# The tail of a diffusion-step kernel: a reciprocal root from ScalarE's square root, and a product on VectorE

## The chip, the cores and the metric

The kernel runs on one core of a Trainium2 chip. A time is the device time of one execution in microseconds (us); a kernel's time is the median of its runs. A core has TensorE (matrix products into PSUM banks), VectorE, ScalarE and GpSimd (element by element, on tiles in SBUF), and SyncE, which issues transfers. Each engine has its own ordered queue of instructions and waits for the others by semaphores. In the profile they are PE, DVE, ACT, POOL and SP; PEld is TensorE's loading of weights.

## The reference

One layer of a diffusion backbone, in float32, for 128 context tokens and 1024 latent tokens with 1024 features. Attention heads and a matrix-memory head group stand side by side, then comes a SwiGLU block of 2816 hidden features, and at the very end a root-mean-square norm with a gain per feature:

```python
def rmsnorm(x, w):
    xf = x.astype(F32)
    y = xf * lax.rsqrt(jnp.mean(xf * xf, axis=-1, keepdims=True) + EPS)
    return (y * w.astype(F32)).astype(x.dtype)
...
    h2 = rmsnorm(x, norm2_w) * (1 + sc2) + sh2
    x = x + g2 * swiglu(h2, w_gu, w_down)
...
y_sample = rmsnorm(xs, final_norm_w)
```

The change touches the last of this, for the last tokens only: the gated sum `x + g2 * ...`, then the sum of its squares over a row, the reciprocal root, and the product with root and gain.

## The kernel before, in words

The 1152 tokens are nine blocks of 128 rows, in three chunks of three blocks (`CB` = 3). A chunk's rows lie in SBUF as `x1[0..2]`, each 128 x 1024. Projections, attention and the matrix memory come first; then each chunk goes through the SwiGLU block in groups of hidden features. For a group, `gate_up` makes 128 hidden features at a time, and `down` multiplies them into the rows and adds the gated result. Each factor is split into a high and a low part, so each product is three matmuls.

For the first two chunks the final norm is done by `finish`, beside the next chunk's matmuls. For the third chunk the last group (four times 128 hidden features) is `down_last`, which ends the program. For each block `i` of its three and each half row `n` of 512 features it does the following:

- twelve matmuls into one PSUM bank (L1391 to L1393);
- `add_gated`: on VectorE the product of the bank with the gate (L1104, `t`), then the sum into the row (L1105, `x`);
- on ScalarE the square of the half row with its sum in a column of `st` (L1397, `jk`; the profile shows a second instruction that reads the accumulator);
- after the first half only: on VectorE one column, sum/1024 + EPS (L1399, `st`), and on GpSimd the half row times the norm's gain `fw` (L1400).

After both halves `rsqrt` (L121 to L134) makes the reciprocal root of the mean square in twelve VectorE operations on one column: L127 forms the mean, L128 and L129 make a first guess from the bits of the number, and three rounds of L131, L132 and L133 are Newton steps. Then ScalarE scales the first half row, which has its gain already (L1403), and VectorE scales the second half and multiplies the gain in one operation (L1404). The first half leaves by a transfer issued from ScalarE's queue (L1405), the second by one from SyncE's (L1406).

The order of the instructions in each engine's queue is made by a planner when the program is built (`TC_OPTS`, L1498). It goes through the program with durations of its own, and lets an engine take what is ready, what stands earlier in the program (or was raised by `hot`) first. So the operations of three blocks are mixed on VectorE, and once the order is made, an engine keeps to it whatever the chip does.

Of the kernel before, what the change touches and what calls it, by code (L numbers as in the profile page):

```python
# [8 lines left out]
F32 = mybir.dt.float32  # L9
# [4 lines left out]
AF = mybir.ActivationFunctionType  # L14
ALU = mybir.AluOpType
# [4 lines left out]
P = 128  # L20
D = 1024
# [12 lines left out]
CB = 3  # L34
# [11 lines left out]
def hybrid_step(ctx: ExitStack, tc: tile.TileContext, I: dict, O: dict):  # L46
    nc = tc.nc
    mm = nc.tensor.matmul
    act = nc.scalar.activation
    dve = nc.vector  # L50
    pool = nc.gpsimd
# [6 lines left out]
    def nm(s):  # L58
        uid[0] += 1
        return f"{s}_{uid[0]}"  # L60
# [24 lines left out]
    def yrow(b):  # L85
        if b == 0:
            return O["y_prompt"][0]
        return O["y_sample"][0, (b - 1) * P : b * P, :]
# [14 lines left out]
    def bank():  # L103
        return psum["mm"].tile([P, 512], F32, name=nm("mm"), tag="mm")
# [16 lines left out]
    def rsqrt(tp, ss, n, inv, cap=16, plus=EPS):  # L121

        v = tp.tile([P, cap], F32, name=nm("rv"), tag="rv", bufs=2)[:, :n]
        y = tp.tile([P, cap], F32, name=nm("ry"), tag="ry", bufs=2)[:, :n]
        t = tp.tile([P, cap], F32, name=nm("rt"), tag="rt", bufs=2)[:, :n]
        h = tp.tile([P, cap], I32, name=nm("rh"), tag="rh", bufs=2)[:, :n]
        dve.tensor_scalar(out=v, in0=ss, scalar1=inv, scalar2=plus, op0=ALU.mult, op1=ALU.add)  # L127
        dve.tensor_scalar(out=h, in0=v.bitcast(I32), scalar1=1, scalar2=None, op0=ALU.logical_shift_right)  # L128
        dve.tensor_scalar(out=y.bitcast(I32), in0=h, scalar1=-1, scalar2=0x5F3759DF, op0=ALU.mult, op1=ALU.add)  # L129
        for _ in range(3):  # L130
            dve.tensor_tensor(out=t, in0=y, in1=y, op=ALU.mult)  # L131
            dve.scalar_tensor_tensor(out=t, in0=t, scalar=-0.5, in1=v, op0=ALU.mult, op1=ALU.mult)  # L132
            dve.scalar_tensor_tensor(out=y, in0=t, scalar=1.5, in1=y, op0=ALU.add, op1=ALU.mult)  # L133
        return y  # L134
# [4 lines left out]
    def load_piece(srcs, shape, raw=None, own=None):  # L139

        a, b = shape
        n = a * b

        def view(t):
            return t[:, :n].rearrange("p (a b) -> p a b", b=b)

        raw = raw or wp.tile([P, 1024], F32, name=nm("raw"), tag="raw", bufs=2)
        hi = own[0] if own else wp.tile([P, 1024], F32R, name=nm("whi"), tag="whi", bufs=5)
        lo = own[1] if own else wp.tile([P, 1024], F32R, name=nm("wlo"), tag="wlo", bufs=5)
        for part, ap_ in srcs:  # L150
            dma(part(view(raw)), ap_)
        nc.scalar.copy(hi[:, :n], raw[:, :n])  # L152
        sub(lo[:, :n], raw[:, :n], hi[:, :n].bitcast(F32), "dve")
        return view(hi), view(lo)
# [162 lines left out]
    for n in (1, 4):  # L317
        dve.tensor_scalar(out=bcol[:, n * KD : (n + 1) * KD], in0=bcol[:, n * KD : (n + 1) * KD],
                          scalar1=1.0, scalar2=None, op0=ALU.add)
# [781 lines left out]
    def add_gated(x1, ps, g, n, eng=dve):  # L1101
        cs = slice(n * 512, (n + 1) * 512)
        t = t2()
        dve.tensor_tensor(out=t, in0=ps, in1=g, op=ALU.mult)  # L1104
        eng.tensor_tensor(out=x1[:, cs], in0=x1[:, cs], in1=t, op=ALU.add)  # L1105
# [248 lines left out]
    def finish(c, a):  # L1354
# [6 lines left out]
        for i in range(CB):  # L1361
# [4 lines left out]
            dma(yrow(c * CB + i), x1[i])  # L1366
            yield

    def down_last(c, a, f0, nf):

        gs, ws = [], []
        fw = ap2.tile([P, D], F32, name="fw", tag="pr", bufs=2)
        dma(fw, I["final_norm_w"].rearrange("(o n) -> o n", o=1).to_broadcast([P, D]))
        for n in range(2):
            pieces = []
            for j in range(0, nf, 2):
                rows = w_down[(f0 + j) * P : (f0 + j + 2) * P, n * 512 : (n + 1) * 512].rearrange("(a p) n -> p a n", p=P)
                pieces.append(load_piece([(full_view, rows)], (2, 512)))
            ws.append(pieces)
            gl = ft.tile([P, 512], F32, name=nm("gl"), tag=("gl", "gx")[n], bufs=1)  # L1380
            dma(gl, g_d[1, 1:2, n * 512 : (n + 1) * 512].to_broadcast([P, 512]))
            gs.append(gl)
        for i in range(CB):
            sl = slice(i * P, (i + 1) * P)
            st = ap.tile([P, 4], F32, name=nm("st"), tag="st", bufs=4)
            for n in range(2):
                ps = bank()
                for k in range(nf):
                    wh, wl = ws[n][k // 2]
                    ah, al = a["act"][k][0][:, sl], a["act"][k][1][:, sl]  # L1390
                    mm(ps, ah, wh[:, k % 2, :], start=(k == 0), stop=False)  # L1391
                    mm(ps, ah, wl[:, k % 2, :], start=False, stop=False)
                    mm(ps, al, wh[:, k % 2, :], start=False, stop=(k == nf - 1))  # L1393
                add_gated(a["x1"][i], ps, gs[n], n)
                v = a["x1"][i][:, n * 512 : (n + 1) * 512]
                jk = ft.tile([P, D], BF16, name=nm("jk"), tag="t2", bufs=3)
                act(jk[:, 0:512], v, AF.Square, accum_out=st[:, n : n + 1])  # L1397
                if n == 0:
                    dve.tensor_scalar(out=st[:, 2:3], in0=st[:, 0:1], scalar1=1.0 / D, scalar2=EPS, op0=ALU.mult, op1=ALU.add)  # L1399
                    pool.tensor_tensor(out=v, in0=v, in1=fw[:, 0:512], op=ALU.mult)  # L1400
            r = rsqrt(fp, st[:, 1:2], 1, 1.0 / D, CB, st[:, 2:3])
            lo, hi = a["x1"][i][:, 0:512], a["x1"][i][:, 512:1024]
            act(lo, lo, AF.Copy, scale=r)  # L1403
            dve.scalar_tensor_tensor(out=hi, in0=hi, scalar=r, in1=fw[:, 512:1024], op0=ALU.mult, op1=ALU.mult)  # L1404
            nc.scalar.dma_start(yrow(c * CB + i)[:, 0:512], lo)  # L1405
            dma(yrow(c * CB + i)[:, 512:1024], hi)  # L1406
# [29 lines left out]
    fp = ctx.enter_context(tc.tile_pool(name="fp", bufs=1, side="right", reuse_waits="tile"))  # L1436
# [31 lines left out]
    for c in range(NCH):  # L1468
        if c + 1 < NCH:
            main = groups(c, cur, GROUPS[:NG])  # L1470
            for _ in range(4):
                next(main)
            weave(main, chain(previous(c, cur), att), 18 * sum(nf for _, nf in GROUPS[:NG]) - 24, 50)
            emit(att)
            attn_out(nxt, oT, out_gates())
            emit(groups(c, cur, GROUPS[NG:-1]))
            f0, nf = GROUPS[-1]
            emit(gate_up(cur, f0, nf))
            n2 = chain(*[norm2(c + 1, nxt, i) for i in range(CB)])
            weave(chain(down(c, cur, f0, nf, 0), down(c, cur, f0, nf, 1)), n2, 6 * nf, 8)  # L1480
            emit(n2)
            if c + 2 < NCH:
                oT = []
                att = attention(c + 2, oT, set())
            nxt["prev"] = cur
            cur = nxt
            nxt = cur["next"] = {}
        else:
            main = groups(c, cur, LAST[:-1])
            for _ in range(4):  # L1490
                next(main)
            weave(main, previous(c, cur), 24, 3)
            emit(main)
            emit(gate_up(cur, *LAST[-1]))
            down_last(c, cur, *LAST[-1])
# [52 lines left out]
```

## Time and profile before

| what | value |
|---|---|
| median of 3 runs | 1572.1 us (1570.31 to 1574.45) |
| the profiled execution, its own time | 1574.08 us |
| its span | 1572.3 us |
| granted TensorE clock, mean | 0.979 |
| busy: TensorE, VectorE, ScalarE, GpSimd | 95%, 65%, 49%, 17% of the span |

The span is the time from the first to the last event of the profile; the execution's own time is 1.8 us longer. A row of the timeline gives start, duration, engine, line of the kernel, operation, and output and input tiles with their shapes. Durations of neighbours on VectorE and ScalarE overlap a little, so the distance from one start to the next is the better measure of what an operation costs its queue. A row in the groups by line ends with busy time, mean nanoseconds of one instruction, and the idle time before them with what ended it.

### The profile page before, as it was taken

The page shows a single profiled execution, that of the slowest core. Times are in us where ns is not written, and L with a number is a line of the kernel's source. Part 1 is how long each engine was busy: PE and PEld are TensorE (multiplying, and loading weights), DVE is VectorE, ACT ScalarE, POOL GpSimd, SP SyncE. Part 2 cuts the span into 40 slices and gives each one's busy share as a digit, 9 for nine tenths or more (in the row PEclk, how much of TensorE's full clock was granted, in tenths as well). Part 3 has the DMA queues.
Part 4 walks back from the last instruction along what each step waited for, and adds up shares of the span by engine and source line. Part 5 has one row for each costly group of instructions (what it writes and reads, how often), then busy time and mean ns, then how long its engine had stood idle before and what let it go on. Part 6 is the DMA issues. An engine that isn't in the chain of part 4 may idle for free.

```text
span 1572.3 us, 23397 instructions
## 1 busy us (share of the span) xinstructions
PE 1487.7 (95%) x8539; PEld 1247.3 (79%) x8539; DVE 1022.9 (65%) x2025; ACT 771.8 (49%) x1409; POOL 271.4 (17%) x357
## 2 busy tenths in 40 slices
PE   6899999999999689999999999999999999999996
PEld 3544567676766468898998989989898989999995
DVE  4878554737659576677555677877866585554555
ACT  4754465847656344545432444556552443323332
POOL 0213333322343242100110101000010101001111
PEclk9899999999999799999999999999999999999998
DMA  9664323523556847767555447878763545544441
GB/s 360 186 182 157 97 68 41 121 47 68 114 150 162 265 80 197 184 174 175 154 154 149 147 126 236 195 170 180 179 162 114 168 133 168 161 130 138 143 139 54
DMA packets 387881, 236.91 MB, mean 151 GB/s; under 512 B 170198, under 2 KB 346790, under 8 KB 387766
## 3 DMA queue, kind: packets, MB, share of 16 engines
q1 hardware_dynamic: 385110, 231.84, 54.1%
q10 hardware_dynamic: 2656, 3.58, 1.1%
q8 instruction: 67, 1.10, 0.3%
q14 instruction: 48, 0.39, 0.1%
HBM read 183.79 MB, written 13.26 MB: 125 GB/s over the span
## 4 chain that ended last, share of the span: by engine, by line
PE 77%; DVE 11%; DMA 5%; ACT 4%; issue 2%; SPq 0%; POOL 0%; ACTq 0%; DVEq 0%; POOLq 0%
PE mm L1316 11%; PE mm L1317 11%; PE mm L1315 11%; PE mm L1115 5%; PE mm L1116 5%; PE mm L1117 5%; PE S L1035 3%; PE wi L483 3%; PE wi L485 3%; PE wi L484 3%; PE mm L116 2%; PE mm L1147 1%; PE mm L1148 1%; PE mm L1149 1%; PE po L1060 1%
## 5 line engine op out<-in xcount | busy, mean ns | idle before, releaser
L152 ACT CAST whi<-raw 128x1024 fp32r<-128x1024 f32 (+1 forms) x216 | 222.3, 1029 | 411.0 <-PE mm L1316 156.5
L137 DVE TENSOR_TENSOR wlo<-raw,whi 128x1024 fp32r<-128x1024 f32 (+1 forms) x216 | 260.4, 1206 | 202.9 <-ACT whi L152 202.3
L1316 PE MATMUL mm<-aTl,whi 128*128 128x384 f32 x1056 | 355.7, 337 | 2.7 <-DVE aTl L137 2.7
L1317 PE MATMUL mm<-aTh,wlo 128*128 128x384 f32 x1056 | 354.3, 336 | 0.0
L1315 PE MATMUL mm<-aTh,whi 128*128 128x384 f32 x1056 | 353.3, 336 | 0.0
L137 POOL TENSOR_TENSOR hl<-tn,hl 128x384 fp32r<-128x384 f32 x66 | 84.4, 1279 | 840.0 <-ACT hl L1338 748.3
L1316 PEld LDWEIGHTS mm<-aTl,whi 128*128 128x128 f32 x1056 | 198.5, 188 | 3.9 <-DVE aTl L137 3.3
L1315 PEld LDWEIGHTS mm<-aTh,whi 128*128 128x128 f32 x1056 | 198.1, 188 | 0.6
L1317 PEld LDWEIGHTS mm<-aTh,wlo 128*128 128x128 f32 x1056 | 198.4, 188 | 0.0
L1116 PE MATMUL mm<-wlo,hl 128*128 128x512 f32 x372 | 145.7, 392 | 0.0
L1115 PE MATMUL mm<-whi,hl 128*128 128x512 f32 x372 | 144.3, 392 | 0.0
L1117 PE MATMUL mm<-whi,hl 128*128 128x512 f32 x372 | 143.4, 392 | 0.0
L483 PE MATMUL wi<-ipair,hT 128*128 128x384 f16 (+2 forms) x408 | 135.6, 335 | 1.7 <-ACT hT L507 1.2
L484 PE MATMUL wi<-ipair,hT 128*128 128x384 f16 (+2 forms) x408 | 135.6, 335 | 0.0
L485 PE MATMUL wi<-ipair,hT 128*128 128x384 f16 (+2 forms) x408 | 132.1, 335 | 1.0 <-DVE hT L137 1.0
L1042 DVE SCALAR_TENSOR_TENSOR pl<-pr,st,ph 128x1152 f16<-128x1152 f32 (+1 forms) x72 | 96.0, 1333 | 31.7 <-ACT ph L1041 31.4
L1037 DVE TENSOR_REDUCE st<-S 128x1 f32<-128x1152 f32 (+1 forms) x72 | 88.9, 1235 | 16.3 <-PE S L1035 16.1
L1038 ACT ACTIVATE pr<-S,st 128x1152 f32<-128x1152 f32 (+1 forms) x72 | 81.3, 1130 | 32.4 <-DVE st L1037 29.3
L1041 ACT ACTIVATE ph<-pr,st 128x1152 f16<-128x1152 f32 (+1 forms) x72 | 83.9, 1165 | 23.8 <-DVE st L1040 6.7
L1035 PE MATMUL S<-kst,qT 128*128 128x384 f32 (+1 forms) x400 | 87.6, 349 | 4.8 <-ACT pr L1038 4.8
L1104 DVE TENSOR_TENSOR t<-mm,gl 128x512 f32<-128x512 f32 x102 | 69.1, 687 | 26.2 <-DMA gl<-g_d 11.5
L1117 PEld LDWEIGHTS mm<-whi,hl 128*128 128x128 f32 x372 | 69.9, 188 | 14.2
(375 smaller groups left out, 2538.4 us busy)
## 6 DMA issues: line engine op xcount, KB each, us to landing
raw<-in_w_gu_dram SPq DMA_DIRECT2D x132, 512.0 KB
raw<-in_w_down_dram SPq DMA_DIRECT2D x60, 512.0 KB
a<-in_w_ada_dram SPq DMA_DIRECT2D x24, 512.0 KB
gl<-g_d SPq DMA_DIRECT2D x36, 256.0 KB
aw<-in_w_ada_dram SPq DMA_DIRECT2D x16, 512.0 KB
iraw<-in_w_in_dram SPq DMA_DIRECT2D x32, 256.0 KB
raw<-in_w_out_dram SPq DMA_DIRECT2D x12, 512.0 KB
x<-in_x_sample_dram SPq DMA_DIRECT2D x11, 512.0 KB
```

What stands on the lines that cost most here:

```text
L137: (dve if eng == "dve" else pool).tensor_tensor(out=out, in0=full, in1=hi, op=ALU.subtract)
L152: nc.scalar.copy(hi[:, :n], raw[:, :n])
L483: mm(ps[:, :n], ah, wh[:, k % 2, c0 : c0 + n], start=(k == 0), stop=False)
L484: mm(ps[:, :n], ah, wl[:, k % 2, c0 : c0 + n], start=False, stop=False)
L485: mm(ps[:, :n], al, wh[:, k % 2, c0 : c0 + n], start=False, stop=(k == KD - 1))
L1035: mm(S[:, n, 0:w], qT[:, h, :], kst[kv][:, t, c0 + n * w : c0 + (n + 1) * w], start=(t == 0), stop=(t == 1))
L1115: mm(ps, ah, wh[:, k % 2, :], start=(k == 0), stop=False)
L1116: mm(ps, ah, wl[:, k % 2, :], start=False, stop=False)
L1117: mm(ps, al, wh[:, k % 2, :], start=False, stop=(k == nk - 1))
L1315: mm(ps, wh[:, k, :], th[:, k, :], start=(k == 0), stop=False)
L1316: mm(ps, wh[:, k, :], tl[:, k, :], start=False, stop=False)
L1317: mm(ps, wl[:, k, :], th[:, k, :], start=False, stop=(k == KD - 1))
```

## The change

A new function `last_rsqrt` takes the place of `rsqrt` in `down_last`, three times in all, once per block. ScalarE takes the square root of the mean square (with `scale` 1/1024 and the column `st[:, 2:3]`, which holds the first half's share plus EPS, as `bias`). VectorE makes the mean square itself, the reciprocal of the root, and one Newton step in three operations. The tile `q` takes its place under the tag `rv`, which `rsqrt` uses for its mean; the result is the fourth column of `st`. The product of the first half row with the gain, L1400, goes from GpSimd to VectorE. Nothing else is changed.

```diff
--- before.py
+++ after.py
@@ -1366,6 +1366,18 @@
             dma(yrow(c * CB + i), x1[i])
             yield
 
+    def last_rsqrt(st):
+
+        q = fp.tile([P, 4], F32, name=nm("lq"), tag="rv", bufs=2)
+        act(q[:, 0:1], st[:, 1:2], AF.Sqrt, scale=1.0 / D, bias=st[:, 2:3])
+        dve.tensor_scalar(out=q[:, 1:2], in0=st[:, 1:2], scalar1=1.0 / D, scalar2=st[:, 2:3], op0=ALU.mult, op1=ALU.add)
+        dve.reciprocal(q[:, 0:1], q[:, 0:1])
+        dve.tensor_tensor(out=q[:, 2:3], in0=q[:, 0:1], in1=q[:, 0:1], op=ALU.mult)
+        dve.scalar_tensor_tensor(out=q[:, 2:3], in0=q[:, 2:3], scalar=-0.5, in1=q[:, 1:2], op0=ALU.mult, op1=ALU.mult)
+        r = st[:, 3:4]
+        dve.scalar_tensor_tensor(out=r, in0=q[:, 2:3], scalar=1.5, in1=q[:, 0:1], op0=ALU.add, op1=ALU.mult)
+        return r
+
     def down_last(c, a, f0, nf):
 
         gs, ws = [], []
@@ -1397,8 +1409,8 @@
                 act(jk[:, 0:512], v, AF.Square, accum_out=st[:, n : n + 1])
                 if n == 0:
                     dve.tensor_scalar(out=st[:, 2:3], in0=st[:, 0:1], scalar1=1.0 / D, scalar2=EPS, op0=ALU.mult, op1=ALU.add)
-                    pool.tensor_tensor(out=v, in0=v, in1=fw[:, 0:512], op=ALU.mult)
-            r = rsqrt(fp, st[:, 1:2], 1, 1.0 / D, CB, st[:, 2:3])
+                    dve.tensor_tensor(out=v, in0=v, in1=fw[:, 0:512], op=ALU.mult)
+            r = last_rsqrt(st)
             lo, hi = a["x1"][i][:, 0:512], a["x1"][i][:, 512:1024]
             act(lo, lo, AF.Copy, scale=r)
             dve.scalar_tensor_tensor(out=hi, in0=hi, scalar=r, in1=fw[:, 512:1024], op0=ALU.mult, op1=ALU.mult)
```

## The prediction

> **What bounds the kernel now.** I read the page first, then the stretches at the end, then the last 22 us instruction by instruction, because the change touches only `down_last`.
>
> ```profile
> span 1572.3 us, 23397 instructions
> ...
> PE 1487.7 (95%) x8539; PEld 1247.3 (79%) x8539; DVE 1022.9 (65%) x2025; ACT 771.8 (49%) x1409; POOL 271.4 (17%) x357
> ...
> PE 77%; DVE 11%; DMA 5%; ACT 4%; issue 2%; SPq 0%; POOL 0%; ACTq 0%; DVEq 0%; POOLq 0%
> ```
>
> TensorE is busy for 95% of the span and carries 77% of the chain that ended last. No edit outside TensorE's path can be worth much, except where TensorE has run dry. The view by stretches finds that place:
>
> ```profile
> core 0: us, PE busy (x) PEld busy (x) DVE busy (x) ACT busy (x) POOL busy (x), PEclk, DMA share, GB/s
> ...
> 1550.50:1559.20 8.70, 8.65 (x39) 6.82 (x37) 8.14 (x15) 2.32 (x7) 2.60 (x2) 1.00 0.00 0
> 1559.20:1568.60 9.40, 0.00 (x0) 0.00 (x0) 8.87 (x40) 4.09 (x9) 1.26 (x1) 0.64 0.29 112
> 1568.60:1572.30 3.70, 0.00 (x0) 0.00 (x0) 0.00 (x0) 0.00 (x0) 0.00 (x0) 0.50 0.37 142
> ```
>
> From 1559.2 us TensorE does nothing. VectorE is busy 8.14 of 8.70 us before that point and 8.87 of 9.40 us after it; then 3.7 us of output transfers remain. So the last 13 us end with VectorE's queue, and the timeline there shows what fills it (columns: start, duration, engine, line, operation, in brackets the idle time before it):
>
> ```profile
> 1550.57 0.69 DVE L1104 TENSOR_TENSOR t<-mm,gl 128x512 f32<-128x512 f32 x1 [6.54 <-PE mm L1393]
> ...
> 1551.30 0.69 DVE L1105 TENSOR_TENSOR x<-x,t 128x512 f32<-128x512 f32 x1
> 1551.51 0.39 PE L1391 MATMUL mm<-whi,hl 128*128 128x512 f32 x1
> ...
> 1551.91 0.69 DVE L1104 TENSOR_TENSOR t<-mm,gl 128x512 f32<-128x512 f32 x1
> ...
> 1552.03 0.63 ACT L1397 ACTIVATE jk<-x 128x512 bf16<-128x512 f32 x1 [7.44 <-DVE x L1105]
> ...
> 1552.78 0.15 DVE L1399 TENSOR_SCALAR st<-st 128x1 f32<-128x1 f32 x1 [0.19 <-ACT jk L1397]
> 1552.83 1.31 POOL L1400 TENSOR_TENSOR x<-x,fw 128x512 f32<-128x512 f32 x1 [7.10 <-ACT jk L1397]
> 1552.86 1.83 DVE L1105 TENSOR_TENSOR x<-x,t 128x512 f32<-128x512 f32 x1
> ...
> 1554.60 0.68 DVE L1104 TENSOR_TENSOR t<-mm,gl 128x512 f32<-128x512 f32 x1
> ...
> 1557.15 1.82 DVE L1105 TENSOR_TENSOR x<-x,t 128x512 f32<-128x512 f32 x1
> ...
> 1558.76 0.39 PE L1393 MATMUL mm<-whi,hl 128*128 128x512 f32 x1
> ...
> 1561.08 0.69 DVE L1104 TENSOR_TENSOR t<-mm,gl 128x512 f32<-128x512 f32 x1
> ...
> 1561.68 1.12 DVE L133 SCALAR_TENSOR_TENSOR ry<-rt,ry 128x1 f32<-128x1 f32 x1
> 1562.72 0.15 DVE L132 SCALAR_TENSOR_TENSOR rt<-rt,rv 128x1 f32<-128x1 f32 x1
> ...
> 1562.86 0.68 DVE L1105 TENSOR_TENSOR x<-x,t 128x512 f32<-128x512 f32 x1
> ...
> 1563.63 0.63 ACT L1397 ACTIVATE jk<-x 128x512 bf16<-128x512 f32 x1 [2.18 <-DVE rt L131]
> ...
> 1564.03 0.75 DVE L1404 SCALAR_TENSOR_TENSOR x<-x,ry,fw 128x512 f32<-128x512 f32 x1
> ...
> 1564.70 0.15 DVE L133 SCALAR_TENSOR_TENSOR ry<-rt,ry 128x1 f32<-128x1 f32 x1
> 1564.77 0.20 DVE L127 TENSOR_SCALAR rv<-st 128x1 f32<-128x1 f32 x1
> ...
> 1566.19 0.16 DVE L132 SCALAR_TENSOR_TENSOR rt<-rt,rv 128x1 f32<-128x1 f32 x1
> ...
> 1566.38 0.16 DVE L133 SCALAR_TENSOR_TENSOR ry<-rt,ry 128x1 f32<-128x1 f32 x1
> ...
> 1567.74 0.75 DVE L1404 SCALAR_TENSOR_TENSOR x<-x,ry,fw 128x512 f32<-128x512 f32 x1
> 1567.80 0.72 ACT L1403 ACTIVATE x<-x,ry 128x512 f32<-128x512 f32 x1 [1.50 <-DVE ry L133]
> 1568.56 0.34 ACTq L1405 DMA_DIRECT2D out_y_sample_dram<-x  x1
> ```
>
> The last matmul starts at 1558.76, so block 2's second half is ready at about 1559.1, but its L1104 starts at 1561.08: VectorE is 2 us behind. From that L1104 to the last scaling (L1404, 1567.74) pass 6.66 us: 1.78 to L1105, 0.77 to Square, 1.14 to L127, 2.97 for the root's twelve small operations, which run one behind the other. Of the backlog, 1.15 us each come from two L1105 that take 1.83 and 1.82 us instead of 0.68, both beside a GpSimd L1400; a third L1400 lies over the L133 at 1561.68 (1.12 instead of 0.15).
>
> **The change part by part.** Prices are steps from one start to the next, because VectorE's operations overlap. A 128x512 operation takes a step of 0.60 (1561.08 to 1561.68), L1404 0.67 (1564.03 to 1564.70), and a dependent 128x512 operation starts 0.73 after its source (1550.57 to 1551.30). A small operation takes 0.07 with other work between (1564.70 to 1564.77), or 0.19 straight behind its source (1566.19 to 1566.38). Square starts 0.73 to 0.77 after its L1105 and releases a VectorE operation 0.75 after its own start (1552.03 to 1552.78).
>
> Product to VectorE. Three GpSimd operations go, and with them the three collisions: the step 1552.86 to 1554.60 (1.74) and its like at 1557.15 shrink to 0.60, and 1561.68 to 1562.72 (1.04) to 0.07: 3.25 off VectorE. Three products come on VectorE at 0.60 each, 1.80, the price of L1105, which also reads two float32 SBUF tensors. Nothing else waits in GpSimd's queue. On VectorE the product sits ahead of the next L1105 if the planner takes it as soon as Square is done; it delays what is behind it by 0.60. Net 1.45 off.
>
> Root on VectorE. Twelve small operations per block become five (reciprocal, the tensor_scalar and three of Newton's step). Reciprocal costs what the others do:
>
> ```profile
> L1039 DVE RECIPROCAL st<-st 128x1 f32<-128x1 f32 x72 | 11.6, 161 | 26.5 <-ACT pr L1038 26.2
> L310 ACT ACTIVATE thc<-cT 128x16 f32<-128x16 f32 x1 | 0.2, 218 | 1.7 <-DVE cT L303 1.7
> ...
> L849 ACT ACTIVATE dt<-mm,QT 128x128 f32<-128x128 f32 x72 | 22.4, 368 | 20.7 <-PE mm L846 20.6
> ...
> L565 ACT ACTIVATE gd<-gc 128x128 f32<-128x128 f32 x1 | 0.3, 311 | 0.0
> ```
>
> For blocks 0 and 1 fourteen operations go that lay between large ones: 14 x 0.07 = 1.0 of VectorE's queue. For block 2 the 2.97 us become Sqrt and four dependent small operations. The trace has no Sqrt. Its bounds are the 16-column activation without pointer operand (0.22) and the 128-column one with a pointer bias (0.37). I take 0.30: 0.22, the 0.06 by which L849 exceeds L565 for the pointer, and 0.02 to hand on. The tensor_scalar (0.20, as L127) hides beside Sqrt; if the tracking of tile `q` made it wait for Sqrt, it would add at most 0.2. So 0.30 + 0.20 + 3 x 0.19 = 1.07, which is 1.9 less than 2.97.
>
> Table load. ScalarE has run one table since the early change to Ln and back:
>
> ```profile
> 103.51 1.28 ACT L564 ACT_TABLE_LOAD   x1
> 104.80 0.31 ACT L564 ACTIVATE gc<-gb 128x128 f32<-128x128 f32 x1
> 105.13 1.28 ACT L565 ACT_TABLE_LOAD   x1
> 106.43 0.31 ACT L565 ACTIVATE gd<-gc 128x128 f32<-128x128 f32 x1
> ```
>
> Each function that the loaded table lacks brings one load of 1.28 (1.29 to the next activation). Ahead of block 0's Sqrt one load must come. It falls at about 1553.9, and the Sqrt that was due then comes at 1555.15. Nothing on ScalarE is late for that, but the reciprocal stands in VectorE's ordered queue, and the L1105 and L1104 of block 1 stand behind it. Bounds: 0, if the planner puts enough large operations ahead of that reciprocal, and 1.29. I take 1.1, near the upper end, because VectorE's planned order in the rows above follows the producer closely. It is paid in the backlog, not in the last chain.
>
> The sum. I placed the new operations by these steps, each engine in order and taking the earliest ready operation, the earlier one in the program on a tie; VectorE is fed at 1550.55, 1551.0, 1551.45, 1553.6, 1556.3 and 1559.1 (33 matmuls of 0.227 from 1551.51 to the end, 12 to a half row). The old operations placed in that way, with 1.15 added to each of three L1105, put the last L1404 at 1567.8, against the row's 1567.74. The new ones give: VectorE idle 1554.3 to 1555.5 (the load), L1105 of block 1's second half at 1556.9, L1104 of block 2's second half at 1560.5, its L1105 at 1561.2 (1562.86 before: 1.7 earlier), Square 1561.9. Under the Square lie block 2's product and block 1's L1404; ScalarE's copy of block 1's first half, placed ahead of Sqrt, delays it to 1563.3. Reciprocal 1563.6, the rest at 1563.8, 1564.0, 1564.2, the last scaling at 1564.4. That is 3.4 us earlier: 1.7 of backlog and 1.7 of the last chain (the 1.9, less 0.6 for Sqrt behind the copy, plus 0.4 by which L127 was late behind other blocks' work: 1.14 after Square's start instead of 0.75).
>
> Outputs. The halves keep their queues. ScalarE's issue of 0.34 now stands ahead of a later Sqrt only if the planner puts it there: 0.3 at most. After the last issue (1568.56) 3.74 us pass to the end, unchanged while blocks 1 and 2 stay apart: 2.2 us before, 1.8 now, for 512 KB that take 1.3 us at the best rate seen:
>
> ```profile
> GB/s 0 0 0 0 0 0 10 0 0 0 0 0 0 0 0 0 0 0 0 0 0 0 0 0 0 0 10 0 0 0 0 355 303 407 206 166 402 67 0 0
> ```
>
> So the profiled execution's 1574.08 becomes 1570.7. It is 2.0 above the median of the runs shown, 1572.1, and within their 1570.31 to 1574.45; the same 3.4 off the median gives 1568.7, which I forecast. 0.3% is 4.7 us, about what a measurement of this kernel can tell from no change, and the gain lies under it.
>
> **The rivals.** First, the load is fully hidden and VectorE catches up with TensorE. The floor is then TensorE's end: 1559.1, + 0.73 + 0.74 + 0.75 + 1.07 = 1562.4, a gain of 5.3; with the load hidden but the same order it is 4.5. Time 1566.8 to 1567.6. For it: 3.25 us of collision are gone. Against: VectorE has no slack of its own until 1559. Chance 0.20.
>
> Second, slower: the table is switched for every block, because Square or Copy is missing from Sqrt's table. ScalarE's order then has six loads (ahead of three Sqrt, of Square in blocks 1 and 2, and of the last copy). Placed in that way the last copy starts at 1568.4, 0.6 later than 1567.80: 1572.7. It decides from about 1.2 us a switch. For it: the trace shows loads at Ln and again at Exp, and no Sqrt table. Against: the load at 105.13 is the last in the trace, and Square and Copy ran beside Exp and Tanh from there to the end. Chance 0.06. The Trainium skill, "ScalarE: Activation LUTs", section "Table sets: the hidden batching unit", has cheap functions such as copy in every set; by that there is one load.
>
> Third, the planner puts block 2's product and block 1's L1404 ahead of the last L1105: 0.60 + 0.67 later, a gain of 2.1, time 1570.0. For it: both stand earlier in the program. Against: they are ready later. Chance 0.16.
>
> Fourth, ScalarE has to run empty before it switches. The longest that can be in its way is a Square, 0.75 to its release; the reciprocal, and with it the backlog, comes that much later: a gain of 2.6, time 1569.5. Against: in the rows above the load at 105.13 starts 0.02 after the activation of 104.80 ends (104.80 + 0.31), and the activation at 106.43 stands 0.02 behind the load. Chance 0.05. The Trainium skill, "ScalarE: Activation LUTs", section "What ACT_TABLE_LOAD costs", gives such a cost as a DRAIN of about 1.38 us on top of the load at every switch, 2.66 us in all; by that the sum would lose 1.4 us, an estimate (1570.1). The rows just named don't show it.
>
> Fifth, the change hardly acts: VectorE waits for the reciprocals of blocks 0 and 1 both (each up to 1.3), the gain is under 1 us, 1571.5. Chance 0.05.
>
> **How the numbers follow.** The forecast (gain 2.5 to 4.4, 1567.7 to 1569.6) has 0.48. The range must hold forecast, third rival and the lower part of the first, with the spread of the runs (about 2 us either way): 1565.6 to 1572.4. Beyond 4.7 us lies half of the first rival and a tail of the forecast: faster 0.17. Slower by 4.7 us needs switches at twice the row's price or another order elsewhere: 0.05. The rest, 0.78, is within 0.3%.
>
> **What would show it.** One ACT_TABLE_LOAD of 1.28 after 1550; no GpSimd work after 1546; L1105 at 0.68 throughout; VectorE idle for some 1 us ahead of the first reciprocal; Square to last scaling about 2.4 us instead of 4.1. The prediction is wrong if there are more loads, if the last L1105 starts after 1562.5, or if the part before 1550 has another order.

## The result, and the profile after

Over 22 runs each, the changed kernel takes 1569.52 us in the median (1567.17 to 1572.62), the kernel before 1572.68 (1569.7 to 1574.77). The ratio of the times is 0.9983, with a 95% interval from 0.9976 to 0.9989: 1.7 to 3.8 us, or 0.11 to 0.24% faster. That is under the 0.3% that the prediction names as about what a measurement can tell, but the interval excludes no change.

The page of the changed kernel:

```profile
span 1566.4 us, 23369 instructions
...
PE 1484.4 (95%) x8539; PEld 1244.8 (79%) x8539; DVE 1017.7 (65%) x2007; ACT 771.7 (49%) x1413; POOL 267.8 (17%) x354
...
PE 80%; DVE 9%; ACT 4%; DMA 4%; issue 2%; POOL 1%; SPq 0%; ACTq 0%; DVEq 0%; POOLq 0%
```

The spans of the two profiled executions (1572.3 and 1566.4) are 5.9 us apart, more than the medians. The end of the program does not make all of that: the first matmul of the last group starts at 1542.63 in the one profile and at 1539.13 in the other. Up to that matmul every engine's queue holds the same instructions in the same order, and other profiles put it elsewhere: a second one of the changed kernel at 1541.02, those of the experiments below between 1538.38 and 1547.20. So I take 3.5 us of the 5.9 to be of the kind that differs from one execution to the next. I therefore use a measure within one profile, the *tail*: from the first L1104 of the last group to the start of the last scaling. It was 1550.57 to 1567.74, 17.17 us, and is 1547.08 to 1561.75, 14.67 us: 2.50 less. A second profile of the changed kernel has 14.67 again (1548.97 to 1563.64).

The three stretches of the prediction (to TensorE's end, to the last issue, to the end of the transfers), except that the second ends here behind the last issue (1562.50 + 0.37) and there at its start (1568.56):

```profile
core 0: us, PE busy (x) PEld busy (x) DVE busy (x) ACT busy (x) POOL busy (x), PEclk, DMA share, GB/s
1547.00:1555.65 8.65, 8.65 (x39) 6.82 (x37) 7.37 (x17) 4.13 (x9) 0.00 (x0) 1.00 0.00 0
1555.65:1562.90 7.25, 0.00 (x0) 0.00 (x0) 6.18 (x20) 4.04 (x11) 0.00 (x0) 0.71 0.38 145
1562.90:1566.40 3.50, 0.00 (x0) 0.00 (x0) 0.00 (x0) 0.00 (x0) 0.00 (x0) 0.50 0.39 150
```

From TensorE's end to the start of the last issue pass 6.85 us (1555.65 to 1562.50) instead of 9.36 (1559.20 to 1568.56). VectorE is busy for 6.18 us of them instead of 8.87, and GpSimd does nothing. From the start of that issue to the end pass 3.90 us, 3.74 before. The timeline of that tail (the line numbers are those of the changed kernel: L1409 is Square, L1412 the product, L1372 Sqrt, L1373 to L1378 the root's VectorE operations, L1415 and L1416 the scalings):

```profile
1547.08 0.69 DVE L1104 TENSOR_TENSOR t<-mm,gl 128x512 f32<-128x512 f32 x1 [6.54 <-PE mm L1405]
...
1549.35 0.68 DVE L1412 TENSOR_TENSOR x<-x,fw 128x512 f32<-128x512 f32 x1
...
1549.95 0.69 DVE L1105 TENSOR_TENSOR x<-x,t 128x512 f32<-128x512 f32 x1
...
1551.41 1.28 ACT L1372 ACT_TABLE_LOAD   x1
...
1552.71 0.30 ACT L1372 ACTIVATE lq<-st 128x1 f32<-128x1 f32 x1
...
1553.04 0.16 DVE L1374 RECIPROCAL lq<-lq 128x1 f32<-128x1 f32 x1 [0.79 <-ACT lq L1372]
...
1554.44 0.68 DVE L1105 TENSOR_TENSOR x<-x,t 128x512 f32<-128x512 f32 x1
...
1557.38 0.67 DVE L1104 TENSOR_TENSOR t<-mm,gl 128x512 f32<-128x512 f32 x1
...
1558.09 0.69 DVE L1412 TENSOR_TENSOR x<-x,fw 128x512 f32<-128x512 f32 x1
1558.69 0.69 DVE L1105 TENSOR_TENSOR x<-x,t 128x512 f32<-128x512 f32 x1
...
1559.41 0.63 ACT L1409 ACTIVATE jk<-x 128x512 bf16<-128x512 f32 x1 [1.93 <-DVE x L1105]
...
1560.04 0.71 ACT L1415 ACTIVATE x<-x,st 128x512 f32<-128x512 f32 x1
...
1560.65 0.28 ACT L1372 ACTIVATE lq<-st 128x1 f32<-128x1 f32 x1
...
1560.96 0.17 DVE L1374 RECIPROCAL lq<-lq 128x1 f32<-128x1 f32 x1 [0.41 <-ACT lq L1372]
...
1561.75 0.75 DVE L1416 SCALAR_TENSOR_TENSOR x<-x,st,fw 128x512 f32<-128x512 f32 x1
...
1562.50 0.37 ACTq L1417 DMA_DIRECT2D out_y_sample_dram<-x  x1
```

The sums (L1105) take 0.68 to 0.69 throughout; 1.83 is gone. One table load comes, at 1551.41, and VectorE stands idle for 0.79 us in front of the first reciprocal, with the sum and product of block 1 behind it. In the last chain, Square to the last scaling takes 2.34 us (1559.41 to 1561.75) instead of 4.11, with 0.5 of it lost where Sqrt waits behind block 1's copy (1560.04).

### The profile page after: what moved, and what is told of

Same layout as the page of the kernel before. It is cut to its first block, busy times and chain, and to the rows that moved or that the text cites. A ratio compares the mean times of both kernels' runs of the same rounds, so it can differ in the third digit from the quotient of the medians.

```text
span 1566.4 us, 23369 instructions
## 1 busy us (share of the span) xinstructions
PE 1484.4 (95%) x8539; PEld 1244.8 (79%) x8539; DVE 1017.7 (65%) x2007; ACT 771.7 (49%) x1413; POOL 267.8 (17%) x354
## 4 chain that ended last, share of the span: by engine, by line
PE 80%; DVE 9%; ACT 4%; DMA 4%; issue 2%; POOL 1%; SPq 0%; ACTq 0%; DVEq 0%; POOLq 0%
PE mm L1316 12%; PE mm L1317 11%; PE mm L1315 11%; PE mm L1115 5%; PE mm L1116 5%; PE mm L1117 5%; PE S L1035 4%; PE wi L485 3%; PE wi L484 3%; PE wi L483 3%; PE mm L1147 2%; PE mm L1148 1%; PE mm L1149 1%; PE mm L116 1%; PE po L1060 1%
## 5 line engine op out<-in xcount | busy, mean ns | idle before, releaser
L1104 DVE TENSOR_TENSOR t<-mm,gl 128x512 f32<-128x512 f32 x102 | 68.9, 685 | 26.2 <-DMA gl<-g_d 12.5
```

## The experiments

All of them ran as timed comparisons with the kernel before, on one chip per group, except the run with the copies on VectorE, which has one time and one profile. A difference of 1 us is at the edge of what the times tell, so the tail decides and the time is given beside it. Each tail comes from one profile; only the changed kernel has two, which agree.

### One part at a time

The first kernel takes the product to VectorE and keeps the old root:

```diff
-            r = last_rsqrt(st)
+            r = rsqrt(fp, st[:, 1:2], 1, 1.0 / D, CB, st[:, 2:3])
```

> The product of the first half row with the gain on VectorE, the old root of twelve VectorE operations. I measure the tail: from the first L1104 of the last group to the start of the last scaling of the last block, 17.17 us before (1550.57 to 1567.74) and 14.67 after (1547.08 to 1561.75). Theory 1, both parts act on VectorE's queue: the three collisions with GpSimd (1.14 + 1.14 + 0.97) go, three products of 0.60 come, and the old root stays; placed by hand with those steps the tail is 15.2, with 0.9 more if the planner puts block 2's product ahead of the last sum as it did after: 15.2 to 16.1, time 1.1 to 2.0 us under before. Theory 2, the root alone makes the gain and the collisions were beside other waits: the tail stays at 17.2 (within 0.3).

Measured: ratio 0.9990 (0.9979 to 1.0000). The tail is 15.61 us, 1.56 less than before. The profile is of the slowest of its runs (1577.19 us), but what was slow there lies ahead of the tail: the first matmul of the last group starts at 1547.20. On VectorE's timeline these are the first and last rows of the tail, and the last sum:

```profile
1555.15 0.69 DVE L1104 TENSOR_TENSOR t<-mm,gl 128x512 f32<-128x512 f32 x1 [6.54 <-PE mm L1405]
...
1565.63 0.69 DVE L1105 TENSOR_TENSOR x<-x,t 128x512 f32<-128x512 f32 x1
...
1570.76 0.75 DVE L1416 SCALAR_TENSOR_TENSOR x<-x,ry,fw 128x512 f32<-128x512 f32 x1
```

The second keeps the new root and leaves the product on GpSimd:

```diff
-                    dve.tensor_tensor(out=v, in0=v, in1=fw[:, 0:512], op=ALU.mult)
+                    pool.tensor_tensor(out=v, in0=v, in1=fw[:, 0:512], op=ALU.mult)
```

> The new root with ScalarE's square root, the product still on GpSimd. Theory 1: the collisions with GpSimd stay (three of about 1.1 us), the table load holds the first reciprocal, and of the root's saving only the last chain's part is left: by hand a tail of 16.8 (16.0 to 17.0), time 0.2 to 1.2 us under before, less than the product alone gives. Theory 2: the root alone makes the gain: tail near 14.7.

Measured: ratio 0.9999 (0.9990 to 1.0008). The tail is 15.80 us (1548.12 to 1563.92), 1.37 less than before. VectorE's timeline has the collisions and the idle time of the load together:

```profile
1548.12 0.69 DVE L1104 TENSOR_TENSOR t<-mm,gl 128x512 f32<-128x512 f32 x1 [6.54 <-PE mm L1405]
...
1550.39 1.81 DVE L1105 TENSOR_TENSOR x<-x,t 128x512 f32<-128x512 f32 x1
...
1554.61 0.16 DVE L1374 RECIPROCAL lq<-lq 128x1 f32<-128x1 f32 x1 [0.80 <-ACT lq L1372]
...
1555.40 1.73 DVE L1105 TENSOR_TENSOR x<-x,t 128x512 f32<-128x512 f32 x1
...
1560.03 0.92 DVE L1375 TENSOR_TENSOR lq<-lq 128x1 f32<-128x1 f32 x1
...
1563.92 0.75 DVE L1416 SCALAR_TENSOR_TENSOR x<-x,st,fw 128x512 f32<-128x512 f32 x1
```

Both parts act, neither alone gives the whole: theory 1. The product alone came within its range. The root alone saved more than forecast (15.80 against 16.0 to 17.0, 16.8 by hand). A part of that miss is the third collision, ahead of the last sum: I had put about 1.1 us for it, and what was held there is a small operation, 0.92 instead of 0.15. That makes some 0.3 of the 1.0 us; the rest I did not take apart. Apart the two save 1.56 + 1.37 = 2.93, together 2.50; why they do not add up is open too. The times are in line with that but could not have shown it: the intervals of both reach 1.

### What the table load costs

One more Sqrt, of one column and with its result unused, stands behind the last cast of hidden features:

```diff
         gs, ws = [], []
+        early = fp.tile([P, CB], F32, name="early", tag="rt", bufs=2)
+        act(early[:, 0:1], a["act"][-1][0][:, 0:1].bitcast(F32), AF.Sqrt, scale=0.0)
         fw = ap2.tile([P, D], F32, name="fw", tag="pr", bufs=2)
```

> As after, with one more square root of one column (of zero times a hidden value) on ScalarE right after the last cast of hidden features, where ScalarE is idle for some 7 us; the one table load goes there. Its result is used nowhere. Theory 1, the load costs because the first reciprocal stands in VectorE's queue: VectorE's idle time of 0.79 us ahead of that reciprocal goes and the tail falls from 14.67 to 13.8 (13.6 to 14.1). Theory 2, the backlog hides the load, since VectorE waits for matmuls later anyway: the tail stays at 14.7 within 0.2.

Measured: tail 13.93 us (1546.33 to 1560.26), 0.74 less than 14.67; ratio to before 0.9983 (0.9974 to 0.9992). The load is at 1540.36 on ScalarE's timeline, and on VectorE's the first reciprocal has no idle time in front of it:

```profile
1540.36 1.28 ACT L1385 ACT_TABLE_LOAD   x1
```

```profile
1551.41 0.15 DVE L1374 RECIPROCAL lq<-lq 128x1 f32<-128x1 f32 x1
...
1557.21 0.68 DVE L1105 TENSOR_TENSOR x<-x,t 128x512 f32<-128x512 f32 x1
...
1559.48 0.17 DVE L1374 RECIPROCAL lq<-lq 128x1 f32<-128x1 f32 x1 [0.41 <-ACT lq L1372]
...
1560.26 0.75 DVE L1418 SCALAR_TENSOR_TENSOR x<-x,st,fw 128x512 f32<-128x512 f32 x1
```

Of 0.79 us of idle time 0.74 reach the end. So the load was not hidden, although ScalarE had room for it: its price was VectorE's wait for the instruction behind it.

### Why the gain was 0.9 us smaller than the sum

Block 2's product is written after its second half's sum, and reads a column of that sum as a scalar which the operation bypasses:

```diff
                 if n == 0:
...
-                    dve.tensor_tensor(out=v, in0=v, in1=fw[:, 0:512], op=ALU.mult)
+                    if i < CB - 1:
+                        dve.tensor_tensor(out=v, in0=v, in1=fw[:, 0:512], op=ALU.mult)
+                elif i == CB - 1:
+                    u = a["x1"][i][:, 0:512]
+                    dve.scalar_tensor_tensor(out=u, in0=u, scalar=v[:, 0:1], in1=fw[:, 0:512], op0=ALU.bypass, op1=ALU.mult)
```

> As after, but block 2's product with the gain is written after its second half's sum and reads a column of that sum as a scalar that the operation bypasses, so that it can't stand ahead of the sum. Theory 1, the prediction's sum was 0.9 us too large because block 2's product stands ahead of the last sum (0.60) and the rest is smaller steps: the last sum comes 0.6 earlier in the tail and the tail falls to 14.1 (13.9 to 14.3). Theory 2, the last sum is held by its matmuls or by another wait: the tail stays at 14.7.

Measured: tail 14.06 us (1547.57 to 1561.63), 0.61 less; ratio 0.9987 (0.9978 to 0.9995). The last sum starts 11.02 us into the tail instead of 11.61, and the product stands behind it:

```profile
1547.57 0.69 DVE L1104 TENSOR_TENSOR t<-mm,gl 128x512 f32<-128x512 f32 x1 [6.54 <-PE mm L1405]
...
1558.59 0.69 DVE L1105 TENSOR_TENSOR x<-x,t 128x512 f32<-128x512 f32 x1
...
1559.31 0.75 DVE L1416 SCALAR_TENSOR_TENSOR x<-x,fw 128x512 f32<-128x512 f32 x1
...
1561.63 0.75 DVE L1420 SCALAR_TENSOR_TENSOR x<-x,st,fw 128x512 f32<-128x512 f32 x1
```

Both steps in one kernel:

> Both single steps together: the table load early, behind the last cast, and block 2's product behind its last sum. Theory 1, the two lie one behind the other in VectorE's queue and add: 14.67 - 0.74 - 0.61 = 13.3 us of tail (13.1 to 13.5), and the time is 3.5 to 4 us under before, about 1.3 under after. Theory 2, the second meets the same slack as the first: 13.9.

Measured: tail 13.32 us (1551.31 to 1564.63).

```profile
1551.31 0.69 DVE L1104 TENSOR_TENSOR t<-mm,gl 128x512 f32<-128x512 f32 x1 [6.54 <-PE mm L1407]
...
1564.63 0.75 DVE L1422 SCALAR_TENSOR_TENSOR x<-x,st,fw 128x512 f32<-128x512 f32 x1
```

The two add up to a hundredth: 14.67 - 0.74 - 0.61 = 13.32. The time did not come as forecast: the medians are 2.2 us apart (1569.49 and 1571.68), not 3.5 to 4, and the ratio is 0.9987 (0.9978 to 0.9996). The times do not tell this kernel from the changed one, and an advantage of 1.35 us is shown by the tail alone.

### Is it ScalarE's copy or VectorE's queue that holds the last root

With the early load, blocks 0 and 1 leave out product and copy; VectorE scales their first halves and multiplies the gain in one operation:

```diff
-                    dve.tensor_tensor(out=v, in0=v, in1=fw[:, 0:512], op=ALU.mult)
+                    if i == CB - 1:
+                        dve.tensor_tensor(out=v, in0=v, in1=fw[:, 0:512], op=ALU.mult)
...
-            act(lo, lo, AF.Copy, scale=r)
+            if i == CB - 1:
+                act(lo, lo, AF.Copy, scale=r)
+            else:
+                dve.scalar_tensor_tensor(out=lo, in0=lo, scalar=r, in1=fw[:, 0:512], op0=ALU.mult, op1=ALU.mult)
```

> As the early load, but blocks 0 and 1 have no product and no copy on ScalarE: VectorE scales their first half rows and multiplies the gain in one operation (0.67 each instead of a product of 0.60). ScalarE has nothing between the last Square and the last Sqrt. Theory 1, the last chain is held by VectorE's queue, not by ScalarE's copy: the last sum comes 0.5 earlier, the reciprocal stays about 2.3 us behind it because block 1's two scalings (1.34) stand ahead of it: tail 13.4 (13.2 to 13.7). Theory 2, as the prediction had it, ScalarE's copy ahead of Sqrt costs 0.6: the reciprocal follows the last sum by 1.7 and the tail is 12.8.

Measured in a single execution: tail 13.55 us (1546.88 to 1560.43), 0.38 less than with the early load alone. Sqrt now starts 0.75 after Square, with nothing between, and its reciprocal still comes 0.97 after it, because two scalings stand ahead of it on VectorE (timeline of all engines):

```profile
1557.22 0.68 DVE L1105 TENSOR_TENSOR x<-x,t 128x512 f32<-128x512 f32 x1
...
1557.94 0.63 ACT L1411 ACTIVATE jk<-x 128x512 bf16<-128x512 f32 x1 [2.59 <-DVE x L1105]
...
1558.21 0.75 DVE L1421 SCALAR_TENSOR_TENSOR x<-x,st,fw 128x512 f32<-128x512 f32 x1
...
1558.69 0.29 ACT L1372 ACTIVATE lq<-st 128x1 f32<-128x1 f32 x1
1558.88 0.74 DVE L1422 SCALAR_TENSOR_TENSOR x<-x,st,fw 128x512 f32<-128x512 f32 x1
...
1559.66 0.15 DVE L1374 RECIPROCAL lq<-lq 128x1 f32<-128x1 f32 x1
```

Theory 1 holds for this kernel: the reciprocal comes 2.44 us after the last sum (1557.22 to 1559.66), with the early load alone 2.27 (1557.21 to 1559.48). The 0.38 us come from the last sum, which stands 0.54 earlier in the tail (10.34 us instead of 10.88). But the edit hands the copies to the very queue that it asks about: block 1's second scaling on VectorE (1558.88) is the copy's replacement. What the copy would cost with nothing in its place, no run shows. In the changed kernel VectorE stands idle for 0.41 us ahead of that reciprocal (1560.96), so an estimate from that row is that some 0.4 us were to be had.

### The price of a switch

A Tanh of one column ahead of each block's last copy, its result unused, forces ScalarE to change tables:

```diff
+            sw = fp.tile([P, CB], F32, name=nm("sw"), tag="rt", bufs=2)
+            act(sw[:, 0:1], r, AF.Tanh)
             act(lo, lo, AF.Copy, scale=r)
```

> As after, with a Tanh of one column on ScalarE ahead of each block's last copy, its result used nowhere, so that ScalarE must switch tables: four loads instead of one in its queue (ahead of block 0's Sqrt, of block 0's Tanh, of block 2's Sqrt and of block 2's Tanh). It prices the prediction's second rival. Theory 1, each load takes 1.28 us and stops ScalarE for no more than that: by hand the second load pushes block 2's first Square and with it the last sum by 1.3, the third the last Sqrt by 1.3, the fourth the last copy by 0.8; the last copy then starts 18.4 us into the tail (17.8 to 19.0), against 17.23 before and 14.67 after: slower than before by 0.6 to 1.8 us. Theory 2, a switch also empties the engine, for another 1.4 us by the Trainium skill, page 'ScalarE: Activation LUTs', section 'What ACT_TABLE_LOAD costs': the distance from the end of the instruction ahead of a load to the start of the one behind it is then 2.7 us and not 1.3, and the tail goes beyond 21.

Measured: the last copy starts 17.81 us into the tail (1547.70 to 1565.51), at the lower end of its range, 0.58 later than before and 3.14 later than after. The ratio is 1.0006 (0.9996 to 1.0016), which leaves open whether the time is longer than before. ScalarE's timeline around the second, third and fourth load:

```profile
1556.54 0.29 ACT L1372 ACTIVATE lq<-st 128x1 f32<-128x1 f32 x1
1556.85 1.28 ACT L1416 ACT_TABLE_LOAD   x1
1558.14 0.20 ACT L1416 ACTIVATE sw<-st 128x1 f32<-128x1 f32 x1
...
1562.50 1.28 ACT L1372 ACT_TABLE_LOAD   x1
...
1563.80 0.29 ACT L1372 ACTIVATE lq<-st 128x1 f32<-128x1 f32 x1
1564.11 1.28 ACT L1416 ACT_TABLE_LOAD   x1
1565.40 0.20 ACT L1416 ACTIVATE sw<-st 128x1 f32<-128x1 f32 x1
1565.51 0.70 ACT L1417 ACTIVATE x<-x,st 128x512 f32<-128x512 f32 x1
```

A load starts 0.02 us behind the instruction ahead of it (1556.54 + 0.29 = 1556.83) and is followed after 1.29: nothing more than its own 1.28, theory 1. Three more loads, with the three Tanh, take more than the change had gained (3.14 against 2.56, both at the last copy, which came 17.23 us into the tail before).

### A version that beats both

The wait that all of these kernels share lies ahead of the tail. Block 0's first half is complete only after some 33 matmuls of the last group, since the planner puts the matmuls of other blocks ahead of block 0's last ones, which need the hidden tile that is made last. With the early load and the late product, the matmuls of blocks 1 and 2 begin with that tile:

```diff
-                for k in range(nf):
+                ks = list(range(nf)) if i == 0 else [nf - 1] + list(range(nf - 1))
+                for k in ks:
...
-                    mm(ps, ah, wh[:, k % 2, :], start=(k == 0), stop=False)
+                    mm(ps, ah, wh[:, k % 2, :], start=(k == ks[0]), stop=False)
...
-                    mm(ps, al, wh[:, k % 2, :], start=False, stop=(k == nf - 1))
+                    mm(ps, al, wh[:, k % 2, :], start=False, stop=(k == ks[-1]))
```

> Both single steps of the run before (early table load, block 2's product late), and the matmuls of blocks 1 and 2 in the last group begin with the fourth hidden feature tile, which is made last, instead of ending with it; so the planner has fewer matmuls to put ahead of block 0's last ones. Block 0's first half is then complete after 27 matmuls of the group, not 33 to 35, some 1.8 us earlier, and VectorE begins that much earlier. I measure from the first matmul of the last group to the start of the last scaling: 25.1 us before (1542.63 to 1567.74), 22.6 after. Theory 1, VectorE's queue is what ends the kernel to the end of its backlog: the 1.3 us of the two steps and most of the 1.8 us come off, until TensorE's own end (1559.1 in the frame of before) and the chain behind it set the end: 20.0 to 20.6. Theory 2, the matmuls' order does not matter because VectorE's backlog comes from later blocks: 21.3 as with the two steps alone.

It ran beside the changed kernel:

> The changed kernel itself, on the same chip and beside the same runs of before as the other kernel of this call, to compare the two: 22.6 us from the first matmul of the last group to the last scaling, time 1.7 to 3.8 us under before.

Measured: 1566.55 us in the median against 1572.08 of before in the same runs, ratio 0.9969 (0.9957 to 0.9982); the changed kernel beside it 1569.49, ratio 0.9994 (0.9984 to 1.0003). For the changed kernel the two comparisons agree poorly: this interval takes in 1 and ends just above the 0.9983 of the first, while the two medians here are 2.6 us apart, as 0.9984 would have them. How large its gain in time is, between 0 and 4 us, the times leave open; its tail is the same to a hundredth. From the first matmul of the last group to the last scaling the new version takes 20.34 us (1539.85 to 1560.19), the changed kernel 22.62 (1541.02 to 1563.64; the first profile has 22.62 as well) and the kernel before 25.11. With the two single steps alone it was 21.26 (1543.37 to 1564.63), so the new order of the matmuls gave 0.92 of the 2.28 us.

```profile
1546.21 0.69 DVE L1104 TENSOR_TENSOR t<-mm,gl 128x512 f32<-128x512 f32 x1 [4.95 <-PE mm L1408]
...
1556.41 0.69 DVE L1104 TENSOR_TENSOR t<-mm,gl 128x512 f32<-128x512 f32 x1 [0.23 <-PE mm L1408]
...
1560.19 0.75 DVE L1423 SCALAR_TENSOR_TENSOR x<-x,st,fw 128x512 f32<-128x512 f32 x1
```

VectorE begins 6.36 us after the group's first matmul instead of 7.95, and the last half row's L1104 at 1556.41 waits for its matmul with 0.23 us of idle time in front: VectorE has caught up with TensorE. What is left is TensorE's end and the chain behind it, 3.78 us from that L1104 to the last scaling; the prediction's floor has 3.29 there (0.73 + 0.74 + 0.75 + 1.07), so some other work still stands in that chain.

## Why the prediction was right, point by point

*Size.* Forecast were 3.4 us less. Measured are 3.16 between the medians, 2.7 by the ratio of the times (interval 1.7 to 3.8), and 2.50 in the tail, which is the lower end of the forecast's 2.5 to 4.4 and lies between the forecast and the third rival's 2.1. So the mechanism was right and the sum too large by 0.9; that the medians come within 0.3 of it is luck, inside the spread of the times. The forecast of 1568.7 stands 0.8 under the measured median, and 0.6 of that is its base: 1572.1 was the median of 3 runs, and 22 give 1572.68.

*Collisions.* Right: with the product on VectorE no sum takes more than 0.69, and the products take a step of 0.60 (1549.35 to 1549.95). The net price of 1.45 for that part compares with 1.56 measured alone.

*The root.* Sqrt takes 0.28 to 0.30, as put; the reciprocal 0.16 to 0.17, as a small operation; Square to last scaling 2.34, put at 2.4. From the last sum to the last scaling it was 4.88 before and is 3.06, 1.82 less, where 1.7 was put. Sqrt stands behind block 1's copy as placed, and the wait there is 0.5 where 0.6 was charged. The run with the copies on VectorE shows that handing the copies to VectorE does not win it back.

*Table load.* One load, as forecast, in front of block 0's Sqrt. VectorE's idle time is 0.79, where 1.1 was taken from bounds of 0 and 1.29, and 0.74 of it reached the end. That it is paid in the backlog and not in the last chain held.

*The term that was mis-sized* is the backlog, "its L1105 at 1561.2 (1562.86 before: 1.7 earlier)". That last sum was 12.29 us into the tail before; it was placed at 10.63 and came at 11.61, so the backlog gave 0.68 and not 1.7. With the 1.82 of the last chain that is the 2.50.

The placement went wrong in the first block already. It has the table load at 1553.9, 3.33 us into its tail; the profile has it 4.33 in. Behind that, the sum of block 1's second half was placed at 1556.9, 6.33 in, and came 7.36 in (1554.44). The rows show what stood there: VectorE took block 0's product (1549.35) ahead of that block's second sum (1549.95, 2.87 in). A load at 1553.9 needs that sum, then 0.73 to Square and 0.75 to its release, by about 1552.4, only 1.8 in, which is before the product even started (2.27 in). The prediction had named this, 0.60 for what is behind a product that is taken as soon as Square is done, but its placement doesn't show it here.

By block 2's last L1104 the profile is only 0.37 behind the placement (10.30 against 9.93); what was made up in between can't be told, since only a few of the placement's times are on record. Then the third rival came true in half: the planner put block 2's product ahead of the last sum, and did not put block 1's scaling there. That is the other 0.61 (1.31 us from L1104 to the sum, placed at 0.7), and the run with the late product gave back just that. A likely reason for the order, which no run tested, is that in these rows a sum starts 0.72 after the L1104 that it reads (1547.08 to 1547.80 in the first block), while VectorE is free after 0.60; in that gap the product was the one that was ready. The planner goes by durations of its own, which the record doesn't have.

*The rivals.* The first (VectorE catches up with TensorE) did not happen in the changed kernel; it took an early load, a late product and another order of matmuls. The second (a switch per block) did not happen. Its price of 0.6 over before was for six loads, and 0.58 was measured with four and three Tanh, so the rival was priced too low if anything; that the two numbers agree is chance. The Trainium skill, "ScalarE: Activation LUTs", section "Table sets: the hidden batching unit", has copy in every set, and the trace agrees: behind the one load at 1551.41 Copy ran at 1560.04 with no load between. Square, which that sentence does not name, did too (1559.41). The fourth (ScalarE runs empty first) is excluded by the 0.02 us ahead of each load. The 2.66 us that the Trainium skill, "ScalarE: Activation LUTs", section "What ACT_TABLE_LOAD costs", names for a switch are not seen here: 1.31 us pass from the end of the instruction ahead of a load to the start of the one behind it (1556.83 to 1558.14). The fifth did not happen: of the reciprocals of blocks 0 and 1, only block 0's was waited for.

## What to carry to other kernels

An ordered queue that is behind, here VectorE's, handed a saved step through to the end nearly one to one (0.74 of 0.79 us, and 0.61 for a product's step of 0.60), and less where another operation then held the end (0.38 of 0.54). So price a change in such a stretch by the queue's steps, and then ask which operation the planner will put into the gaps between an operation and its dependent. An instruction that is cheap on its own engine, such as a table load on an idle ScalarE, costs what the engine behind it waits; give it a place before the stretch. And where executions differ by several us, a measure within one profile decides what times can't.

## What the runs showed of the hardware that I had not expected

The tail repeats far better than the time: 14.67 us twice, and two single savings of 0.74 and 0.61 that add to 1.35, while times of one kernel spread over 5 us (1567.17 to 1572.62). And a GpSimd operation does not hold only large VectorE operations: the 0.92 us at 1560.03 with the root alone, like the 1.12 of before, is an operation on one column, 0.15 elsewhere. In both profiles it ends with GpSimd's operation, to 0.01 us (before: 1561.53 + 1.26 and 1561.68 + 1.12; with the root alone: 1559.68 + 1.27 and 1560.03 + 0.92). So the two were, as the profile has it, held for the rest of GpSimd's operation, and the difference between them is when they started in it.
